# Four matmuls behind the MLP norm's mean, and a new order of the first loads, in a decoder trunk

## The chip, the cores and the metric

One core of a Trainium2 chip runs the whole kernel. Its engines are TensorE (PE, matmuls; PEld, its weight loads), VectorE (DVE), ScalarE (ACT), GpSimd (POOL) and SyncE (SP). Transfers between DRAM and SBUF are issued from the queues of SP, ACT and POOL. The metric is the device time of one execution in microseconds, lower is better, as the median of several runs.

## The reference

Two layers over 512 tokens of width 1024, in float32. Each layer is a mixer (latent attention in the first, gated linear attention in the second) and an MLP with a squared ReLU, each behind an RMS norm and added to the residual stream. The MLP is where most of the time goes:

```python
def rms_norm(x, gain):
    xf = x.astype(jnp.float32)
    y = xf * lax.rsqrt(jnp.mean(xf * xf, axis=-1, keepdims=True) + EPS)
    return (y * gain.astype(jnp.float32)).astype(x.dtype)
...
def sq_relu_mlp(xn, w_up, w_down):
    hid = jnp.square(jax.nn.relu(xn @ w_up))
    return hid @ w_down
...
for i in range(DEPTH):
    xn = rms_norm(x, norm_mix[i])
...
    x = x + mix.astype(x.dtype)
    x = x + sq_relu_mlp(rms_norm(x, norm_mlp[i]), mlp_w_up[i], mlp_w_down[i]).astype(x.dtype)
return rms_norm(x, final_norm)
```

w_up is 1024 x 4096 and w_down 4096 x 1024. The first projection of the attention layer multiplies the normed x by columns of `mla_w_in`.

## The kernel before

**Precision.** Every large product is made of three passes in the float32r format: each operand is split into a high part (ACT copies it with rounding, line 112) and a low part (DVE subtracts the high part, line 115). `mm3` (lines 120 to 122) is high x high, low x high and high x low with 512 moving columns; the MLP's `matmuls` (line 826) does the same with 256 columns. Each weight piece thus takes a transfer, an ACT split and a DVE subtraction before TensorE can use it.

**The start.** The end of `trunk_kernel` issues the first transfers: the gains, the weights of the latent projection in four parts of 256 KB (`raw0`, named wraw_ckv in the profile, by `load_part`), and x in eight tiles of 128 x 512 (256 KB each, by `load_x`, named xT). Some stand in SP's queue and some in ACT's. Eight counters are shared by the transfers of these two queues, so the ninth transfer in the program's order waits for the landing of the first, and so on. `exp_set` (line 127) loads ACT's function table. Fifteen matmuls on a tile of ones (line 1599, two passes each) come first on TensorE. The program's order is kept for ACT's splits: one weight part, then the two x tiles that go with it (line 245 makes the high part of x times its gain, line 246 on DVE the low part). The product over k = 0 to 7 uses x tile k with weight part k // 2, and TensorE takes the k in order. The product behind it needs the next weight transfer (wraw, 1 MB).

**The MLP.** `mlp` is a generator. Its first part runs while the projection ahead of it ends. Then it builds both matrix products by a seven-product scheme over 2 x 2 blocks: `up_block(b)` yields steps (`s1` with the product named 11, `s2` with 21, `s5` with T1 and so on), and `down_block` yields products over the hidden tiles. A list in `mlp` sets which step follows which. Moving operands are x0 to x7 (high `x0h`, low `x0l`), the combinations T0 to T3, and h, the split hidden tiles. Weights are wh and wl (three buffers each); for block 1's product 11 the pieces are the tiles w, which lie in the space of T3.

Where these tiles lie matters for the reading of the profile. In the program as built, the byte address within a partition, modulo 512, is 96 for all x and T tiles and for w, 416 for wh and wl, and 352 for h. An h1 tile is shifted by 40 elements for that, except the first of each down block, which stays unshifted at 192:

```python
h = dp.tile([P, 8 * TH + 40], F32R, tag="h1", name=uname("h"))
c = 0 if turn[1] != s else 40
h = h[:, c : c + 8 * TH].rearrange("p (i k t) -> p i k t", i=2, k=4)
```

Below, the offset of a matmul is the address of its moving tile less that of its weights, modulo 512 bytes. Two matmuls of offset 0, whose result is never read, already stand at the MLP's begin:

```python
x = quad["11"][0][0]
PE.matmul(t[:, h * TH : (h + 1) * TH], x[:, :P], x, start=h == 0, stop=True, skip_group_check=True)
```

**The norm.** The mean of squares is one float32 matmul with a constant matrix (`nrm.mean`, line 255, tile acc), kept in program order between block 1's product 11 and block 0's product 21. `nrm.finish` makes the reciprocal root from it, which the products need only at their evacuation.

Of the kernel before, what the change touches and what calls it, by code (L numbers as in the profile page):

```python
# [10 lines left out]
F32 = mybir.dt.float32  # L11
# [7 lines left out]
P = 128  # L19
# [6 lines left out]
TH = S // 2  # L26
# [23 lines left out]
def trunk_kernel(ctx: ExitStack, tc: tile.TileContext, t_in: dict, out: bass.AP, out_row: bass.AP):  # L50
    nc = tc.nc
    PE, ACT, DVE, POOL, SP = nc.tensor, nc.scalar, nc.vector, nc.gpsimd, nc.sync
# [6 lines left out]
    def opened(name, side="left", space=None):  # L59
        es = ExitStack()  # L60
        kw = {"space": space} if space is not None else {"side": side}
        now[name] = es, es.enter_context(tc.tile_pool(name=uname(name), bufs=1, reuse_waits="tile", **kw))
        return now[name][1]
# [4 lines left out]
    def pool_of(name):  # L68
        return now[name][1]
# [3 lines left out]
    def uname(s):  # L73
        count[0] += 1
        return f"{s}_{count[0]}"

    def bank(tag):
        if "mps" in now:
            return pool_of("mps").tile([P, 512], F32, tag="u", bufs=3, name=uname("ps"))
        return pool_of("ps").tile([P, 512], F32, tag=f"ps_{tag}", bufs={"a": 2, "b": 3, "c": 3}[tag], name=uname("ps"))  # L80
# [29 lines left out]
    def split(src, hi, lo, hi_eng=ACT, lo_eng=DVE, order=lambda i: i):  # L110
        if hi_eng is ACT:
            raised.append(order(ACT.activation(hi, src, AF.Copy)))  # L112
        else:
            hi_eng.tensor_copy(hi, src)
        return lo_eng.tensor_tensor(lo, src, f(hi), ALU.subtract)  # L115
# [10 lines left out]
    def exp_set():  # L126
        table[0] = tc.keep_in_program_order(ACT.preload_act_table_set("natural_log_exp_and_others"))
# [17 lines left out]
    def piece(raw, a, n, order=lambda i: i):  # L145
        hi = sb.tile([P, a, n], F32R, tag="wh", bufs=3, name=uname("wh"))
        lo = sb.tile([P, a, n], F32R, tag="wl", bufs=3, name=uname("wl"))
        cut_at.append(split(raw, hi, lo, order=order))
        return hi, lo
# [13 lines left out]
    xall = const.tile([P, ND, S], F32, name="xT")  # L163
    xT = [xall[:, j] for j in range(ND)]
    x_in = t_in["x"].rearrange("(j p) t -> p j t", p=P)

    def load_x(q, j):
        q.dma_start(xall[:, j], x_in[:, j])

    eps_t = const.tile([P, 1], F32, name="eps_t")  # L170
    DVE.memset(eps_t, EPS)
# [637 lines left out]
    def mlp(layer, nrm, nxt, final=False):  # L809
# [342 lines left out]
        mp = opened("mps", space=bass.MemoryType.PSUM)  # L1152
# [4 lines left out]
        for n, (m0, tk) in {2: (0, first), 3: (0, second), 4: (KH, first), 5: (KH, second)}.items():  # L1157
            acc[n] = xall[:, m0 : m0 + KH, tk]

        t = mp.tile([P, 512], F32, tag="seed", name=uname("ps"))  # L1160
        for h in range(2):
            x = quad["11"][0][0]
            PE.matmul(t[:, h * TH : (h + 1) * TH], x[:, :P], x, start=h == 0, stop=True, skip_group_check=True)
        for b in range(2):
            wide[b] = halves(wide_raw())
        for b, t in enumerate(halves(wide_raw())):
            fills[b](t)
        kept = tc.keep_in_program_order
        for b in range(2):
            blocks[b].pop(0)()  # L1170
        t = nrm.combine(KH - 1, dp.tile([P, 4, TH], F32, tag="q", bufs=6, name=uname("q")))
        kept(nrm.mean())
        made[1]["21"] = piece(made[1]["a12"], KH, 256)
        kept(cut_at[-1])
        kept(nrm.combined(KH - 1, t))
# [399 lines left out]
    raw0 = pool_of("stage").tile([P, ND, 256], F32, tag="wraw", bufs=2, name="wraw_ckv")  # L1575
    src0 = t_in["mla_w_in"][0][:, QL : QL + KL].rearrange("(k p) n -> p k n", p=P)

    def load_part(k0, k1):
        SP.dma_start(raw0[:, k0:k1], src0[:, k0:k1])

    ACT.dma_start(gains, t_in["gains"])
    load_part(0, 2)
    load_x(ACT, 0)
    load_x(SP, 1)
    load_x(ACT, 2)
    load_part(2, 4)
    load_x(ACT, 3)
    load_part(4, 6)
    load_x(ACT, 4)
    load_x(SP, 5)  # L1590
    load_part(6, 8)
    load_x(SP, 6)
    load_x(SP, 7)
    POOL.dma_start(pos_i, t_in["positions"])
    POOL.dma_start(invf, t_in["inv_freq"].to_broadcast([P, 32]))
    exp_set()
    warm = bank("c")
    for _ in range(15):
        PE.matmul(warm[:, :P], ones128, ones128, start=True, stop=True)
    w0 = []  # L1600
    for k0, k1 in ((0, 2), (2, 4), (4, 6), (6, 8)):
# [40 lines left out]
    n_mix1 = Mixer(ND, inv_d, "mix", ND, "A")  # L1642
    n_mlp0 = mlp_norm(0)
    mlp0 = mlp(0, n_mlp0, n_mix1)
    out_proj(t_in["mla_w_o"][0], O, n_mlp0, mlp0, begun)
    next(mlp0, None)
# [5 lines left out]
    class Final:  # L1652
# [39 lines left out]
        def row(self, t, c, p):  # L1692
# [19 lines left out]
            for eng, q, cs in ((ACT, ACT, slice(0, 384)), (DVE, SP, slice(384, D))):  # L1712
# [4 lines left out]
                q.dma_start(o[:, cs], y[:, cs])  # L1717

    mlp1 = mlp(1, n_mlp1, Final(), True)
    out_proj(t_in["gla_w_o"][0], Y, n_mlp1, mlp1)  # L1720
    next(mlp1, None)
# [23 lines left out]
def build(nc, shapes):  # L1745
    args = {}
    for name, (shape, dt) in shapes.items():
        args[name] = nc.dram_tensor(f"in_{name}_dram", shape, dt, kind="ExternalInput").ap()
    o = nc.dram_tensor("out_0_dram", (D, TH), F32, kind="ExternalOutput").ap()
    o_row = nc.dram_tensor("out_1_dram", (TH, D), F32, kind="ExternalOutput").ap()  # L1750
    with tile.TileContext(nc) as tc:
        trunk_kernel(tc, args, o, o_row)
# [22 lines left out]
```

## Time and profile before

| | |
|---|---|
| Median of 3 runs | 1066.10 us (1065.54 to 1068.97) |
| The profiled execution's own time | 1065.53 us |
| Its span, first to last instruction | 1063.8 us |
| TensorE busy | 1055.4 us, 99% |
| VectorE busy | 856.6 us, 81% |
| ScalarE busy | 642.4 us, 60% |
| Mean granted TensorE clock | 0.998 |
| First MLP's two spare matmuls, its mean | at 189.39 us, at 195.24 us |
| Second MLP's mean | at 742.27 us |

Time stamps are microseconds from the span's start. In a timeline row stand the start, the duration, the engine, the line, the operation, the result tile and its inputs (buffer numbers left out), the shapes, and how many like instructions the row merges; brackets hold the idle time before it and what ended it. Matmuls are pipelined: a record lasts longer than its step, so the pace is read from start to start, or from the number of matmuls in a stretch.

### The profile page before, as it was taken

The page shows a single profiled execution, that of the slowest core. Times are in us where ns is not written, and L with a number is a line of the kernel's source. Part 1 is how long each engine was busy: PE and PEld are TensorE (multiplying, and loading weights), DVE is VectorE, ACT ScalarE, POOL GpSimd, SP SyncE. Part 2 cuts the span into 40 slices and gives each one's busy share as a digit, 9 for nine tenths or more (in the row PEclk, how much of TensorE's full clock was granted, in tenths as well). Part 3 has the DMA queues.
Part 4 walks back from the last instruction along what each step waited for, and adds up shares of the span by engine and source line. Part 5 has one row for each costly group of instructions (what it writes and reads, how often), then busy time and mean ns, then how long its engine had stood idle before and what let it go on. Part 6 is the DMA issues. An engine that isn't in the chain of part 4 may idle for free.

```text
span 1063.8 us, 17962 instructions
## 1 busy us (share of the span) xinstructions
PE 1055.4 (99%) x7332; PEld 975.8 (92%) x7332; DVE 856.6 (81%) x1186; ACT 642.4 (60%) x937; POOL 78.8 (7%) x104
## 2 busy tenths in 40 slices
PE   9999999999999999999999999999999999999997
PEld 7788988999999999988788888888999999999986
DVE  6789879899799789967565654678999799799965
ACT  6577645575667777644334734655665667776734
POOL 7400001000000000030000000001000000000000
PEclk9999999999999999999999999999999999999999
DMA  7312017765553663360222211238665555654412
GB/s 219 91 50 80 7 34 217 165 193 145 173 141 118 179 155 112 99 203 26 53 77 80 80 59 61 80 99 218 179 141 154 158 126 159 173 127 117 139 40 79
DMA packets 114946, 127.81 MB, mean 120 GB/s; under 512 B 8640, under 2 KB 86736, under 8 KB 114864
## 3 DMA queue, kind: packets, MB, share of 16 engines
q1 hardware_dynamic: 98832, 108.15, 32.0%
q0 software_dynamic: 13792, 16.80, 10.2%
q10 hardware_dynamic: 2240, 1.73, 0.5%
q8 instruction: 57, 0.93, 0.4%
q14 instruction: 25, 0.20, 0.1%
HBM read 124.56 MB, written 2.10 MB: 119 GB/s over the span
## 4 chain that ended last, share of the span: by engine, by line
PE 96%; DVE 2%; ACT 0%; DMA 0%; issue 0%; ACTq 0%; DVEq 0%
PE ps L826 51%; PE ps L120 13%; PE ps L122 13%; PE ps L121 13%; PE ps L1426 2%; PE ps L137 1%; PE ps L1465 0%; PE ps L1432 0%; PE ps L1412 0%; PE ps L685 0%; PE ps L686 0%; PE ps L684 0%; PE ps L682 0%; PE ps L683 0%; DVE stat L695 0%; DMA gains<-in_gains_dram 0%
## 5 line engine op out<-in xcount | busy, mean ns | idle before, releaser
L112 ACT ACTIVATE wh<-raw 128x1024 fp32r<-128x1024 f32 x208 | 219.8, 1060 | 152.7 <-PE ps L826 99.4
L115 DVE TENSOR_TENSOR wl<-raw,wh 128x1024 fp32r<-128x1024 f32 x208 | 251.8, 1220 | 25.4 <-ACT wh L112 25.1
L826 PE MATMUL ps<-h,wh 128*128 128x256 f32 x1344 | 168.6, 278 | 0.0
L826 PEld LDWEIGHTS ps<-h,wh 128*128 128x128 f32 x1344 | 161.2, 188 | 0.0
L120 PE MATMUL ps<-set,wh 128*128 128x512 f32 x232 | 91.3, 394 | 0.0
L826 PE MATMUL ps<-h,wl 128*128 128x256 f32 x672 | 91.2, 278 | 0.0
L121 PE MATMUL ps<-set,wh 128*128 128x512 f32 x232 | 90.7, 391 | 0.1
L122 PE MATMUL ps<-set,wl 128*128 128x512 f32 x232 | 90.7, 391 | 0.0
L112 ACT ACTIVATE wh<-wraw 128x1024 fp32r<-128x1024 f32 x41 | 43.1, 1057 | 74.2 <-PE ps L122 41.5
L826 PEld LDWEIGHTS ps<-h,wl 128*128 128x128 f32 x672 | 83.6, 188 | 0.0
L879 POOL DMA_DIRECT2D raw<-in_mlp_w_up_dram x20 | 25.8, 1290 | 707.4 <-DMA raw<-in_mlp_w_up_dram 330.5
L891 ACT ACTIVATE q<-q 128x512 f32<-128x512 f32 x64 | 40.3, 630 | 40.2 <-DVE q L890 39.8
L115 DVE TENSOR_TENSOR h<-q,h 128x1024 fp32r<-128x1024 f32 x44 | 53.7, 1222 | 9.1 <-ACT h L112 9.0
L120 PE MATMUL ps<-wh,set 128*128 128x512 f32 x144 | 59.7, 414 | 0.0
L115 DVE TENSOR_TENSOR wl<-wraw,wh 128x1024 fp32r<-128x1024 f32 x41 | 50.3, 1226 | 11.1 <-ACT wh L112 10.8
L122 PE MATMUL ps<-wh,set 128*128 128x512 f32 x144 | 56.3, 391 | 0.0
L121 PE MATMUL ps<-wl,set 128*128 128x512 f32 x144 | 56.2, 390 | 0.0
L121 PEld LDWEIGHTS ps<-set,wh 128*128 128x128 f32 x232 | 43.6, 188 | 9.9 <-DVE set L246 0.9
L122 PEld LDWEIGHTS ps<-set,wl 128*128 128x128 f32 x232 | 43.6, 188 | 9.4 <-DVE wl L115 0.5
L120 PEld LDWEIGHTS ps<-set,wh 128*128 128x128 f32 x232 | 43.5, 188 | 9.0 <-issue 0.2
L112 ACT ACTIVATE h<-q 128x1024 fp32r<-128x1024 f32 x44 | 46.0, 1049 | 0.2
L121 PE MATMUL ps<-hl,wh 128*128 128x512 f32 x96 | 37.4, 389 | 0.0
(512 smaller groups left out, 2789.4 us busy)
## 6 DMA issues: line engine op xcount, KB each, us to landing
raw<-in_mlp_w_down_dram SPq DMA_DIRECT2D x38, 1024.0 KB, 5.2
raw<-in_mlp_w_up_dram SPq DMA_DIRECT2D x70, 512.0 KB, 5.3
wraw<-in_gla_w_in_dram SPq DMA_DIRECT2D x11, 1024.0 KB, 5.1
raw<-in_mlp_w_up_dram POOLq DMA_DIRECT2D x20, 512.0 KB, 7.4
raw<-in_mlp_w_down_dram POOLq DMA_DIRECT2D x6, 1024.0 KB, 9.3
wraw<-in_mla_w_o_dram SPq DMA_DIRECT2D x8, 512.0 KB, 4.8
wraw<-in_gla_w_o_dram SPq DMA_DIRECT2D x8, 512.0 KB, 4.7
wraw_qn<-in_mla_w_uq_dram SPq DMA_DIRECT2D x6, 256.0 KB, 3.4
```

What stands on the lines that cost most here:

```text
L112: raised.append(order(ACT.activation(hi, src, AF.Copy)))
L115: return lo_eng.tensor_tensor(lo, src, f(hi), ALU.subtract)
L120: PE.matmul(psum, wh, xh, start=start, stop=False, **kw)
L121: PE.matmul(psum, wh, xl, start=False, stop=False, **kw)
L122: PE.matmul(psum, wl, xh, start=False, stop=stop, **kw)
L137: PE.transpose(psum, src, ident[: src.shape[0], : src.shape[0]])
L826: return PE.matmul(p[:, m * TH : (m + 1) * TH], w[i][:, k - k0, m * P : (m + 1) * P], x[k][j], start=start, stop=stop, skip_group_check=True,)
L879: POOL.dma_start(t, rows(half, trail), accum_op=ALU.add)
L891: ACT.activation(qs, qs, AF.Square)
L1426: PE.matmul(p[:, t * 64 : (t + 1) * 64].rearrange("p (n c) -> p n c", c=m), k[:, sl], later, start=True, stop=True)
```

## The change

It does four things. Behind the mean of each MLP, four more matmuls of offset 0 on x0h go into an unused PSUM tile (`spare`, kept in program order). The last six x tiles are loaded in pairs, three transfers of 512 KB, one from ACT's queue and two from SP's; weight part 4 to 6 goes from SP's queue to ACT's. The function table's load moves ahead, between ACT's first x transfer and its second. The matmuls on ones go from 15 to 14.

```diff
@@ -164,8 +164,8 @@
     xT = [xall[:, j] for j in range(ND)]
     x_in = t_in["x"].rearrange("(j p) t -> p j t", p=P)
 
-    def load_x(q, j):
-        q.dma_start(xall[:, j], x_in[:, j])
+    def load_x(q, j, n=1):
+        q.dma_start(xall[:, j : j + n], x_in[:, j : j + n])
 
     eps_t = const.tile([P, 1], F32, name="eps_t")
     DVE.memset(eps_t, EPS)
@@ -1157,19 +1157,24 @@
         for n, (m0, tk) in {2: (0, first), 3: (0, second), 4: (KH, first), 5: (KH, second)}.items():
             acc[n] = xall[:, m0 : m0 + KH, tk]
 
-        t = mp.tile([P, 512], F32, tag="seed", name=uname("ps"))
-        for h in range(2):
+        def spare(t, n):
             x = quad["11"][0][0]
-            PE.matmul(t[:, h * TH : (h + 1) * TH], x[:, :P], x, start=h == 0, stop=True, skip_group_check=True)
+            for h in range(n):
+                i = PE.matmul(t[:, h * TH : (h + 1) * TH], x[:, :P], x, start=h % 2 == 0, stop=True, skip_group_check=True)
+                if n > 2:
+                    kept(i)
+
+        kept = tc.keep_in_program_order
+        spare(mp.tile([P, 512], F32, tag="seed", name=uname("ps")), 2)
         for b in range(2):
             wide[b] = halves(wide_raw())
         for b, t in enumerate(halves(wide_raw())):
             fills[b](t)
-        kept = tc.keep_in_program_order
         for b in range(2):
             blocks[b].pop(0)()
         t = nrm.combine(KH - 1, dp.tile([P, 4, TH], F32, tag="q", bufs=6, name=uname("q")))
         kept(nrm.mean())
+        spare(mp.tile([P, 4 * TH], F32, tag="d", bufs=2, name=uname("ps")), 4)
         made[1]["21"] = piece(made[1]["a12"], KH, 256)
         kept(cut_at[-1])
         kept(nrm.combined(KH - 1, t))
@@ -1575,27 +1580,24 @@
     raw0 = pool_of("stage").tile([P, ND, 256], F32, tag="wraw", bufs=2, name="wraw_ckv")
     src0 = t_in["mla_w_in"][0][:, QL : QL + KL].rearrange("(k p) n -> p k n", p=P)
 
-    def load_part(k0, k1):
-        SP.dma_start(raw0[:, k0:k1], src0[:, k0:k1])
+    def load_part(k0, k1, q=SP):
+        q.dma_start(raw0[:, k0:k1], src0[:, k0:k1])
 
     ACT.dma_start(gains, t_in["gains"])
     load_part(0, 2)
     load_x(ACT, 0)
     load_x(SP, 1)
-    load_x(ACT, 2)
+    exp_set()
+    load_x(ACT, 2, 2)
     load_part(2, 4)
-    load_x(ACT, 3)
-    load_part(4, 6)
-    load_x(ACT, 4)
-    load_x(SP, 5)
+    load_part(4, 6, ACT)
+    load_x(SP, 4, 2)
     load_part(6, 8)
-    load_x(SP, 6)
-    load_x(SP, 7)
+    load_x(SP, 6, 2)
     POOL.dma_start(pos_i, t_in["positions"])
     POOL.dma_start(invf, t_in["inv_freq"].to_broadcast([P, 32]))
-    exp_set()
     warm = bank("c")
-    for _ in range(15):
+    for _ in range(14):
         PE.matmul(warm[:, :P], ones128, ones128, start=True, stop=True)
     w0 = []
     for k0, k1 in ((0, 2), (2, 4), (4, 6), (6, 8)):
```

TensorE at the mean of the first MLP; ps with a number is the PSUM tile, acc the sum of squares, w, x and wh as above. Before:

```order
L826 MATMUL ps_2303<-x1h_2030,w_2172 128x256 x2
L826 MATMUL ps_2303<-x2h_2118,w_2172 128x256 x2
L826 MATMUL ps_2303<-x3h_2226,w_2172 128x256 x2
L255 MATMUL ps_2336<-acc_1947,inv_101 128x512
L826 MATMUL ps_2274<-x4h_1950,wh_2163 128x256
L826 MATMUL ps_2274<-x4l_1951,wh_2163 128x256
```

Now:

```order
L826 MATMUL ps_2299<-x1h_2026,w_2168 128x256 x2
L826 MATMUL ps_2299<-x2h_2114,w_2168 128x256 x2
L826 MATMUL ps_2299<-x3h_2222,w_2168 128x256 x2
L255 MATMUL ps_2332<-acc_1943,inv_101 128x512
L1163 MATMUL ps_2334<-x0h_1939 128x256 x4
L826 MATMUL ps_2270<-x4h_1946,wh_2159 128x256
L826 MATMUL ps_2270<-x4l_1947,wh_2159 128x256
```

The four stand between the mean and product 21; all other matmuls of the MLP keep their order and their addresses modulo 512.

ACT at the start. Before:

```order
L1581 DMA gains<-in_gains_dram 128x51
L168 DMA xT<-in_x_dram 128x512 x4
L127 ACT_TABLE_LOAD
L112 ACTIVATE wh_149<-wraw_ckv 128x512
L245 ACTIVATE set_153<-xT,gains 128x512
L245 ACTIVATE set_157<-xT,gains 128x512
```

Now:

```order
L1586 DMA gains<-in_gains_dram 128x51
L168 DMA xT<-in_x_dram 128x512
L127 ACT_TABLE_LOAD
L168 DMA xT<-in_x_dram 128x2x512
L1584 DMA wraw_ckv<-in_mla_w_in_dram 128x2x256
L112 ACTIVATE wh_145<-wraw_ckv 128x512
L245 ACTIVATE set_149<-xT,gains 128x512
```

The table load is ahead of the pair x2 and x3. The transfer that waits for the landing of the gains is now a weight part instead of x4; ACT's splits keep their order.

SP at the start. Before:

```order
L1579 DMA wraw_ckv<-in_mla_w_in_dram 128x2x256
L168 DMA xT<-in_x_dram 128x512
L1579 DMA wraw_ckv<-in_mla_w_in_dram 128x2x256 x2
L168 DMA xT<-in_x_dram 128x512
L1579 DMA wraw_ckv<-in_mla_w_in_dram 128x2x256
L168 DMA xT<-in_x_dram 128x512 x2
L142 DMA wraw_321<-in_mla_w_in_dram 128x8x256
```

Now:

```order
L1584 DMA wraw_ckv<-in_mla_w_in_dram 128x2x256
L168 DMA xT<-in_x_dram 128x512
L1584 DMA wraw_ckv<-in_mla_w_in_dram 128x2x256
L168 DMA xT<-in_x_dram 128x2x512
L1584 DMA wraw_ckv<-in_mla_w_in_dram 128x2x256
L168 DMA xT<-in_x_dram 128x2x512
L142 DMA wraw_317<-in_mla_w_in_dram 128x8x256
```

Two transfers of x became pairs, one weight part left the queue, and the 1 MB weight transfer (wraw) is the seventh of this queue instead of the ninth. Only the second pair and wraw still wait for a landing (that of the first weight part and that of x0).

## The prediction

> **What bounds the kernel now.** I read the page first (engines, then the chain that ended last).
>
> ```profile
> PE 1055.4 (99%) x7332; PEld 975.8 (92%) x7332; DVE 856.6 (81%) x1186; ACT 642.4 (60%) x937; POOL 78.8 (7%) x104
> PE 96%; DVE 2%; ACT 0%; DMA 0%; issue 0%; ACTq 0%; DVEq 0%
> ```
>
> TensorE is never off for long, so the end can move in only two ways: the matmuls follow each other faster, or the short start and the few stalls shrink. Busy time cannot show the first, because a busy TensorE need not run at its best pace. So I asked for the matmuls of the MLP (line 826, all 128x256) stretch by stretch.
>
> ```profile
> 197.00:238.00 41.00, 41.00 (x350) 41.00 (x349) 1.00 0.60 160
> 247.00:325.00 78.00, 78.00 (x664) 78.00 (x663) 1.00 0.58 160
> 335.00:390.00 55.00, 55.00 (x488) 55.00 (x487) 1.00 0.50 140
> 400.00:460.00 60.00, 60.00 (x532) 60.00 (x531) 1.00 0.41 121
> 744.00:785.00 41.00, 41.00 (x350) 41.00 (x350) 1.00 0.60 160
> 882.00:936.00 54.00, 54.00 (x479) 54.00 (x478) 1.00 0.53 147
> ```
>
> Columns: stretch, length, busy TensorE and number of matmuls, busy weight loads, granted clock, DMA. A record lasts 0.28 us and one that reaches into a stretch is counted, so a step is (length + 0.28) / count: 78.28 / 664 = 117.9 ns in the second row, 60.28 / 532 = 113.3 ns in the fourth. Same line, shape, granted clock (1.00) and full occupation, and two paces, 4.5 ns apart. The first MLP runs at 117.9 ns up to about 332 us and at 113.3 after it; the second repeats it (41.28 / 350 = 117.9, then 54.28 / 479 = 113.3). Each pace holds for tens of microseconds: it is a state that something sets. The timeline of TensorE shows where.
>
> ```profile
> 189.39 0.40 PE L1163 MATMUL ps<-x0h 128*128 128x256 f32 x2
> 189.62 0.28 PE L826 MATMUL ps<-x0h,wh 128*128 128x256 f32 x1
> 190.09 0.28 PE L826 MATMUL ps<-x1h,wh 128*128 128x256 f32 x1
> 190.54 0.28 PE L826 MATMUL ps<-x2h,wh 128*128 128x256 f32 x1
> ...
> 192.36 0.28 PE L826 MATMUL ps<-x0h,w 128*128 128x256 f32 x1
> 192.84 0.28 PE L826 MATMUL ps<-x1h,w 128*128 128x256 f32 x1
> ...
> 195.24 1.02 PE L255 MATMUL ps<-acc,inv 128*128 128x512 f32 x2
> 195.69 0.68 PE L826 MATMUL ps<-x4h,wh 128*128 128x256 f32 x1
> 196.21 0.28 PE L826 MATMUL ps<-x4l,wh 128*128 128x256 f32 x1
> 196.56 0.28 PE L826 MATMUL ps<-x5h,wh 128*128 128x256 f32 x1
> 197.03 0.28 PE L826 MATMUL ps<-x6h,wh 128*128 128x256 f32 x1
> ```
>
> Four matmuls lie between the starts of x1h and x2h: (190.54 - 190.09) / 4 = 113 ns, the fast pace, right behind the two spare matmuls of line 1163. In the product with the tile w a step is (192.84 - 192.36) / 4 = 120 ns. Behind the mean (line 255) it is (197.03 - 196.56) / 4 = 118 ns, and so it stays. I sort matmuls by the offset between the addresses of their moving tile and their weights, modulo 512 bytes, as the build assigns them: 0 for line 1163 and for the product with w, 192 for x and T against wh or wl, 448 for an ordinary h, 288 for the first h1 tile of a down block, which `operand` leaves unshifted. What the rows show: offset 0 draws to 120 ns; offsets 192 and 448 run at 113.3 or 117.9, whichever they were left in; and the entry behind the mean leaves the slow one. The pace turns once more:
>
> ```profile
> 331.20 0.63 PE L826 MATMUL ps<-h,wl 128*128 128x256 f32 x4
> 331.67 0.28 PE L826 MATMUL ps<-x4h,wh 128*128 128x256 f32 x1
> 332.13 0.28 PE L826 MATMUL ps<-x5h,wh 128*128 128x256 f32 x1
> ...
> 396.54 0.74 PE L826 MATMUL ps<-h,wl 128*128 128x256 f32 x5
> 397.12 0.28 PE L826 MATMUL ps<-x4h,wh 128*128 128x256 f32 x1
> 397.60 0.28 PE L826 MATMUL ps<-x5h,wh 128*128 128x256 f32 x1
> ```
>
> Those unshifted h1 blocks of 48 products stand at 238.5 to 244.1, 326.1 to 331.7 and 391.5 to 397.1. Entered slow, the first ends slow and the second ends fast. The third is entered fast and ends fast. They run at 5.6 us / 48 = 117 ns in either state.
>
> **The change part by part: the mean.** Four matmuls of offset 0, on x0h as weights and moving tile, go behind the mean of each MLP. They wait for nothing (x0h was read at 189.39, the PSUM tile is unused), and nobody reads them. Cost: 4 x 120 ns (the w rows) = 0.48 us in each MLP, 0.96 together, all on TensorE's path. DVE and ACT meanwhile go on with the weights that come next.
>
> What they bring is a state, and no row shows this very sequence, so I bound it. At worst the state stays slow: nothing gained. At best everything from 196.6 to 331.7 runs fast: 135.1 us less the two unshifted blocks of 5.6 each = 123.9 us / 117.9 ns = 1051 matmuls x 4.5 ns = 4.7 us in each MLP, 9.4 together. I take the fast end. The nearest rows are those at 189.39: two matmuls of offset 0, then offset 192, and the pace is fast. The mean itself only ends late (the start of 196.21 less one step is 196.09), so the first of the four starts like any matmul behind a stall. A fast entry into the first unshifted block then resembles the third block, which ends fast.
>
> [...]
>
> Can DVE and ACT keep up?
>
> ```profile
> 196.00:240.00 44.00, 44.00 (x374) 43.91 (x373) 40.67 (x42) 29.34 (x38) 1.28 (x1) 1.00 0.62 163
> ```
>
> DVE has 40.67 us of work there. At the fast pace the 44 us become 44 x 113.3 / 117.9 = 42.3, so DVE would be 96% full: tight, but below full, and the four matmuls give it 0.48 us of lead. I cost this at nothing; uncovered, it is a rival below.
>
> **The start.** Queues, table load and warm-up are one term, since they feed one chain: transfers, ACT, DVE, TensorE.
>
> ```profile
> 4.22 1.28 ACT L127 ACT_TABLE_LOAD   x1 [4.22 <-DMA gains<-in_gains_dram]
> 5.52 0.63 ACT L112 ACTIVATE wh<-wraw_ckv 128x512 fp32r<-128x512 f32 x1
> 6.05 1.33 ACT L245 ACTIVATE set<-xT,gains 128x512 fp32r<-128x512 f32 x2
> 8.10 0.71 ACT L245 ACTIVATE set<-xT,gains 128x512 fp32r<-128x512 f32 x1
> 10.06 0.73 ACT L245 ACTIVATE set<-xT,gains 128x512 fp32r<-128x512 f32 x1 [1.25 <-DMA xT<-in_x_dram]
> ...
> 5.90 0.94 PE L1599 MATMUL ps<-ones 128*128 128x128 f32 x7
> 6.81 0.73 PE L120 MATMUL ps<-set,wh 128*128 128x512 f32 x2
> 17.70 0.39 PE L120 MATMUL ps<-set,wh 128*128 128x512 f32 x1
> 18.60 0.39 PE L121 MATMUL ps<-set,wh 128*128 128x512 f32 x1
> 19.03 0.50 PE L122 MATMUL ps<-set,wl 128*128 128x512 f32 x1
> ...
> 10.82 0.75 DVE L246 SCALAR_TENSOR_TENSOR set<-xT,gains,set 128x512 fp32r<-128x512 f32 x1 [1.10 <-ACT set L245]
> 17.66 2.70 DVE L115 TENSOR_TENSOR wl<-wraw,wh 128x1024 fp32r<-128x1024 f32 x2 [1.74 <-ACT wh L112]
> ...
> 7.00:8.00 1.00, 0.94 (x4) 0.46 (x4) 1.00 (x2) 0.82 (x2) 0.00 (x0) 1.00 0.54 58
> 9.00:10.00 1.00, 1.00 (x6) 0.81 (x5) 0.71 (x2) 0.00 (x0) 0.42 (x1) 1.00 1.07 401
> ```
>
> ACT's last x transfer waits for the landing of the gains, the table load follows it, and the first split follows that at 5.52. Now the table load runs during that wait; behind the wait ACT issues one weight transfer (some 0.4 us) and can split at about 4.3. Then it needs x0, which is in by 6.05 at the latest. One warm-up matmul less (two passes; 0.91 us for the seven from 5.90 to 6.81, so 0.13 each) takes the other bound of the first product back by 0.26: TensorE begins some 0.3 us earlier. SP issues two transfers fewer and no longer stands behind x's landings before its third weight transfer; what lands when is still set by the bytes ahead in the queues. The first product needs x in order, and x2 now shares one transfer, and one landing, with x3. Before, x2 was in by 8.10 and x3 only by 10.06: in ACT's queue the same bytes stand ahead of x3's end, and the hole at 7 to 8 us (58 GB/s against 401 two microseconds later) lies in front of it. So x2 lands with x3, at about 10.0. Then ACT takes 0.73, DVE 0.75, and TensorE gets x2's low part at 11.5. From there stand 35 matmuls of this product (one of x2's six done, five blocks of six behind) and two of the next; a step is (18.60 - 17.70) / 4 = 0.225 us, so 37 x 0.225 = 8.3, and the matmul that starts at 19.03 today starts at 19.8: +0.8 us. If the transfer lands a microsecond sooner, that matmul only waits for wl (17.66 + 1.35) as it does now, and the start costs nothing. The low end, -0.3, has that weight transfer sooner too and takes TensorE's whole earlier beginning; the high end, +1.3, has x2 at 10.5. I take +0.8, since x3's row is the nearest.
>
> The Trainium skill ("DMA: Bandwidth & Descriptors", section "Issuing engines are not separate DMA queues") says that transfers from ACT and SP share the same 16 engines and that a second issuing queue saves issue time only. The 401 GB/s with both queues full agrees: moving a weight transfer to ACT's queue brings no bandwidth.
>
> **Sum.** Against the profiled run: 1065.5 - 9.4 + 1.0 + 0.8 = 1057.9. That run lies 0.6 under the median of 1066.1, so I forecast 1058.5 for a median.
>
> **Rivals.**
> - The state stays slow behind the four matmuls, or pace is set by columns alone. For it: the stall at the mean leaves slow today. Against: offset 0 led to fast at 189.39. Time: 1066.1 + 1.0 + 0.8 = 1067.9, no measurable change.
> - Fast only until the first unshifted block, whose end at 244.1 was slow although 331.7 and 397.1 were fast. Gain 42 us less the four matmuls, 41.5 / 117.9 ns x 4.5 ns = 1.6 per MLP: 1066.1 - 3.2 + 1.8 = 1064.7.
> - The other side: the slow state survives, and its new phase makes the second and third unshifted blocks end slow too, as the first does today. Place: 331.7. Then 332 to 462 us, less one block, also runs slow: 124 us / 113.3 ns x 4.5 ns = 4.9 per MLP: 1067.9 + 9.8 = 1077.7. It decides as soon as the matmuls behind 331.7 step at 118 ns.
> - DVE becomes the bound between 196 and 332 us and eats half: 1058.5 + 4.7 = 1063.2.
>
> **Chances.** Fast throughout 0.70 (own range 1056.5 to 1060.5: start -0.3 to +1.3, a few tenths to one microsecond lost to DVE); fast to the first block 0.09; state unchanged 0.12; slow beyond 0.06; DVE 0.03. A measurement here tells 0.3%, 3.2 us, from no change. Faster: the first and half of the last, 0.72. Same: 0.09 + 0.12 + 0.01 = 0.22. Slower: 0.06. A range to 1065.5 takes in the partial cases and leaves out the unchanged and the slower one.
>
> **What the changed profile would show.** Between 197 and 238 us line 826 at 113.3 ns (about 364 matmuls in 41 us) and no turn at 332; the same behind the second mean; four rows at line 1163 of 115 to 120 ns each behind line 255. The first x2 set of ACT behind a DMA wait at about 10 us, and TensorE idle then. Wrong: 117.9 ns behind the mean, or DVE as releaser of weight loads there; a start gain, if x2's set stands near 8 us.

## The result, and the profile after

The changed kernel takes 1059.2 us (median of 6 runs, 1058.46 to 1061.33) against 1065.88 us before on the same chip: ratio 0.9937, 95% interval 0.9922 to 0.9952. That is 6.7 us or 0.6% less, 0.7 us more than the 1058.5 forecast. The profiled execution took 1058.69 us.

The page's first part and its chain look like before's: TensorE is as full, and there is just less of it.

```profile
PE 1047.2 (99%) x7338; PEld 967.7 (92%) x7338; DVE 855.7 (81%) x1186; ACT 640.9 (61%) x937; POOL 78.8 (7%) x104
PE 96%; DVE 2%; DMA 1%; issue 0%; ACT 0%; ACTq 0%; DVEq 0%
```

Six more matmuls in all, and 8.2 us less busy time. Line 826 stretch by stretch, columns as in the prediction:

```profile
197.00:238.00 41.00, 40.48 (x358) 40.60 (x359) 1.00 0.63 163
247.00:325.00 78.00, 78.00 (x690) 78.00 (x689) 1.00 0.60 161
335.00:390.00 55.00, 55.00 (x487) 55.00 (x486) 1.00 0.52 139
400.00:460.00 60.00, 59.35 (x524) 59.16 (x522) 1.00 0.38 115
744.00:785.00 41.00, 41.00 (x363) 41.00 (x363) 1.00 0.55 158
882.00:936.00 54.00, 54.00 (x478) 54.00 (x477) 1.00 0.59 152
```

The second row had 664 matmuls and has 690, the fifth had 350 and has 363: 78.28 / 690 = 113.4 ns and 41.28 / 363 = 113.7. The rows behind 332 us were fast already and stay so. (The first row starts ahead of the first product; the fourth ends behind the last one.) TensorE's timeline at the first mean:

```profile
195.94 0.40 PE L826 MATMUL ps<-x3h,w 128*128 128x256 f32 x2
196.18 1.02 PE L255 MATMUL ps<-acc,inv 128*128 128x512 f32 x2
196.64 1.04 PE L1163 MATMUL ps<-x0h 128*128 128x256 f32 x4
197.52 0.28 PE L826 MATMUL ps<-x4h,wh 128*128 128x256 f32 x1
197.99 0.28 PE L826 MATMUL ps<-x5h,wh 128*128 128x256 f32 x1
198.44 0.28 PE L826 MATMUL ps<-x6h,wh 128*128 128x256 f32 x1
198.89 0.28 PE L826 MATMUL ps<-x7h,wh 128*128 128x256 f32 x1
```

The four spares take 0.88 us, of which about 0.40 is the mean's late end, which x4h's first matmul bore before. Behind them the steps are (197.99 - 197.52) / 4 = 118 ns once, and then (198.89 - 198.44) / 4 = 113: the pace is fast after four matmuls, and no later block of offset 288 ends it. DVE in the tightest stretch:

```profile
196.00:240.00 44.00, 44.00 (x384) 43.52 (x384) 40.96 (x43) 30.01 (x39) 1.27 (x1) 1.00 0.65 167
```

DVE is 93% full, and no weight load between 197 and 332 us waits for it.

The start, first ACT's timeline:

```profile
4.37 0.63 ACT L112 ACTIVATE wh<-wraw_ckv 128x512 fp32r<-128x512 f32 x1 [1.28 <-DMA wraw_ckv<-in_mla_w_in_dram]
6.03 1.33 ACT L245 ACTIVATE set<-xT,gains 128x512 fp32r<-128x512 f32 x2 [1.03 <-DMA xT<-in_x_dram]
10.00 1.33 ACT L245 ACTIVATE set<-xT,gains 128x512 fp32r<-128x512 f32 x2 [2.12 <-DMA xT<-in_x_dram]
```

TensorE's two waits in its timeline:

```profile
10.78 0.50 PE L120 MATMUL ps<-set,wh 128*128 128x512 f32 x1 [0.62 <-ACT set L245]
11.56 0.50 PE L121 MATMUL ps<-set,wh 128*128 128x512 f32 x1 [0.29 <-DVE set L246]
```

And two windows (length; busy TensorE, weight loads, DVE, ACT, POOL; clock; DMA share, GB/s):

```profile
7.00:8.00 1.00, 0.94 (x5) 0.46 (x4) 1.00 (x2) 0.88 (x2) 0.00 (x0) 1.00 1.19 54
9.00:12.00 3.00, 2.09 (x9) 1.19 (x8) 1.24 (x2) 1.33 (x2) 1.81 (x4) 1.00 1.06 388
```

The first split stands at 4.37, not 5.52, but then ACT waits for x0 to 6.03 and the first product begins at 6.80 as before. x2's set waits for the pair to 10.00, and TensorE is idle 0.91 of the 3 us from 9 to 12. The hole of 54 GB/s is still there.

Matched matmul by matmul with before, TensorE is 0.96 us late at 20 us and stays so up to the mean; each set of four spares adds 0.47 net; the first MLP then gains 4.65 us between 197 and 332, the second 4.66. The last matmul is 7.4 us earlier. Behind it the changed kernel takes 0.55 us longer. The larger part is a wait in DVE's last small steps (in its timeline, before and then now):

```profile
1058.85 0.15 DVE L1708 SCALAR_TENSOR_TENSOR sm<-sm 128x1 f32<-128x1 f32 x1
1059.12 0.22 DVE L1709 SCALAR_TENSOR_TENSOR sm<-sm,sm 128x1 f32<-128x1 f32 x1
```

```profile
1051.45 0.15 DVE L1710 SCALAR_TENSOR_TENSOR sm<-sm 128x1 f32<-128x1 f32 x1
1052.07 0.22 DVE L1711 SCALAR_TENSOR_TENSOR sm<-sm,sm 128x1 f32<-128x1 f32 x1 [0.47 <-DVE sm L1710]
```

The step from one to the other takes 0.62 us instead of 0.27; the rest lies behind the issue of the last output transfers. This is not chance from run to run. From the last matmul's start to the span's end, the seven profiled kernels with the old loads take 6.60 to 6.61 us, and the six with the new loads of x and of the weight parts take 7.17 to 7.21. So it goes with the new loads, although nothing in this part of the program was edited; how they reach it was not tried. Sum: 0.96 + 0.94 - 9.31 + 0.55 = -6.86, against 1058.69 - 1065.53 = -6.84.

### The profile page after: what moved, and what is told of

It reads as the page before. It is cut to its first block, busy times and chain, and to the rows that moved or that the text cites. A ratio compares the mean times of both kernels' runs of the same rounds, so it can differ in the third digit from the quotient of the medians.

```text
span 1057.0 us, 17970 instructions
## 1 busy us (share of the span) xinstructions
PE 1047.2 (99%) x7338; PEld 967.7 (92%) x7338; DVE 855.7 (81%) x1186; ACT 640.9 (61%) x937; POOL 78.8 (7%) x104
## 4 chain that ended last, share of the span: by engine, by line
PE 96%; DVE 2%; DMA 1%; issue 0%; ACT 0%; ACTq 0%; DVEq 0%
PE ps L826 51%; PE ps L120 13%; PE ps L121 13%; PE ps L122 13%; PE ps L1431 2%; PE ps L137 1%; DMA xT<-in_x_dram 1%; PE ps L1470 0%; PE ps L1437 0%; PE ps L1417 0%; PE ps L685 0%; PE ps L686 0%; PE ps L682 0%; PE ps L684 0%; PE ps L683 0%; DVE stat L695 0%
```

## The experiments

Each is timed against the kernel before on the same chip, in three groups of four; before was 1066.01, 1065.76 and 1066.05 us in them.

### The two halves apart

**spares_only:** the kernel before, with `spare` and its two calls as in the diff above.

> The kernel before with the four matmuls behind each mean and nothing else. By position in the program, the changed kernel's TensorE falls 0.96 us behind at the start and then gains 8.35 us in the two MLPs (4.65 us each, less 0.47 us for the four matmuls). Theory (the spares carry the whole gain and the start costs): 1065.9 - 8.3 = 1057.6 us, 1.5 us faster than the full change; line 826 at 113.3 ns between 197 and 238 us, and x2's set near 8 us. Rival (the two traces' start differs only from run to run, or the new start helps): 1059.2 us or more, the same as the full change.

Measured: 1057.62 us (1057.29 to 1058.07), ratio 0.9918 (0.9905 to 0.9931). Line 826 in its trace:

```profile
247.00:325.00 78.00, 78.00 (x690) 78.00 (x690) 1.00 0.59 161
744.00:785.00 41.00, 41.00 (x363) 41.00 (x363) 1.00 0.55 155
```

The eight matmuls alone bring 8.4 us, more than the whole change. Its start is before's, and yet its TensorE is 0.52 us later at 20 us than in before's profiled run. So the start varies from run to run: at that point the other profiled kernels with before's start unaltered stand from 0.09 us ahead of it (before_h1_448) to 0.38 (spares_448) and 0.60 us (two_spares_448) behind it. Against the mean of these five, the new start costs some 0.7 us there, not 0.96.

**start_only:** the changed kernel without the second call.

```diff
         kept(nrm.mean())
-        spare(mp.tile([P, 4 * TH], F32, tag="d", bufs=2, name=uname("ps")), 4)
```

> The changed kernel without the four matmuls: queues, pairs, table load and warm-up alone. Theory: the start costs what it cost in the full change, 0.96 us at the matmul that waited for wl at 19.03 us before: 1066.8 us; 117.9 ns behind the mean. Rival (the start is worth nothing or a gain): 1065.9 us or below.

Measured: 1068.77 us, ratio 1.002 (1.0012 to 1.0029). Line 826 in its trace:

```profile
197.00:238.00 41.00, 41.00 (x348) 40.97 (x348) 1.00 0.63 161
247.00:325.00 78.00, 78.00 (x665) 78.00 (x663) 1.00 0.61 162
```

The slow pace, as before. The start is a loss. The profiled run (1067.06) is 1.5 us over before's: 0.93 at the last matmul and 0.59 behind it, as in the changed kernel. By the median the loss is larger: three of the 11 runs lie at 1067.1 to 1067.2, eight at 1068.2 to 1070.7. What can make that difference shows in the next experiment.

### What sets the pace behind the mean

**spares_at_192:** the changed kernel, the spares' weights 80 elements further on.

```diff
             x = quad["11"][0][0]
+            c = 80 if n > 2 else 0
...
-                i = PE.matmul(..., x[:, :P], x, ...)
+                i = PE.matmul(..., x[:, c : c + P], x, ...)
```

> The changed kernel with the weights of the four spares taken 80 elements further on in x0h, so that their offset is 192 like that of the products around them; number, shape, place and operands' tile stay. Theory (offset 0 moves the phase between weight load and matmul): the state stays slow, 117.9 ns up to 332 us, 1059.2 + 9.3 = 1068.5 us. Rival (any four matmuls between the mean and product 21 do it, by taking up the stall or the weights): 1059.2 us.

Measured: 1062.21 us (1061.9 to 1064.54), ratio 0.9964 (0.9952 to 0.9975): between the two. Line 826:

```profile
197.00:238.00 41.00, 39.84 (x339) 39.74 (x338) 1.00 0.62 151
247.00:325.00 78.00, 78.00 (x690) 78.00 (x689) 1.00 0.62 162
```

At the mean the theory holds: four matmuls of the same tile, shape and place, but of offset 192, leave the pace at 117.8 ns (41 us less the part ahead of the first product). Then the first block of offset 288, which ended slow before, ended fast. That turn I had not expected here.

The same profiled run, taken at 1064.54 us, shows the start's second cost: TensorE's wait for x2 in its timeline.

```profile
11.85 0.49 PE L120 MATMUL ps<-set,wh 128*128 128x512 f32 x1 [1.79 <-ACT set L245]
```

The windows behind it, columns as above:

```profile
13.00:14.00 1.00, 1.00 (x4) 0.81 (x3) 0.79 (x2) 1.00 (x3) 0.92 (x3) 0.53 1.09 354
14.00:15.00 1.00, 1.00 (x3) 0.73 (x3) 1.00 (x3) 1.00 (x3) 1.00 (x2) 0.50 1.05 338
15.00:16.00 1.00, 1.00 (x4) 0.79 (x3) 1.00 (x2) 1.00 (x3) 0.86 (x2) 0.50 0.69 230
16.00:17.00 1.00, 1.00 (x5) 0.82 (x4) 1.00 (x2) 0.42 (x1) 0.97 (x2) 0.77 0.07 24
```

x2 came 1.1 us later than in the changed kernel's profiled run, TensorE stood idle for 1.79 us, and from about 13.1 to 16.5 the granted clock was 0.50: 3.4 us at half pace, 1.7 us lost. one_spare and three_at_192, with the same start, show it too (idle 1.66 and 1.99 of the 3 us from 9 to 12, clock 0.50 at 14 to 15); the kernel before, the changed kernel's profiled run (idle 0.91) and start_only's (0.36) do not. The two groups of runs of start_only, and the changed kernel's two runs at 1060.7 and 1061.3 beside four at 1058.5 to 1059.5, are some 2 us apart, which fits. Those runs have no profile, but the mean granted clock of each run is on record: in start_only 0.998 to 0.999 in the three and 0.996 to 0.998 in the eight, where 3.4 us at half would take 0.0016. The old start is not free of it either, by the same sign: two of before's 20 runs in this group, at 1068.8 and 1069.5 us, have 0.997. The Trainium skill ("TensorE: Matmul & The Clock Gate", section "HAM oscillation — how this bites in real kernels") asks for no idle gap over some 3.4 us. Here the clock fell 1.2 us behind a gap of 1.79 us, so the measurement decides.

**one_spare:** the changed kernel with `spare(..., 1)`.

> The changed kernel with one spare matmul instead of four behind each mean. In the changed trace the start of the weight load ahead of each matmul stands 115, 116, 117 and 118 ns before its matmul from the second spare to the first product of 21: each product of offset 0 adds 1 ns, and the kernel before stays slow at 114.5. Theory (the phase must be carried past about 116): with one spare the first product meets 115 ns as before, the state stays slow: 1059.2 + 9.3 - 0.7 = 1067.8 us. Rival (one matmul of offset 0 is enough to set the state): 1059.2 - 0.7 = 1058.5 us.

Measured: 1062.99 us (1061.49 to 1065.73), ratio 0.9967 (0.9955 to 0.9978). By the trace the same picture as with four at 192: slow behind the mean (x350 in 744:785), the first block of offset 288 ends fast (x690 in 794:872). One spare does not set the pace, as the theory said; the time was 4.8 us under its number because that block ended fast, which brings 2 x 690 x 4.44 ns = 6.1 us, and the half clock, which its profiled run shows, takes up to 1.7 of it back.

**two_spares_448:** spares_448 (below) with two spares.

> Old start, every h1 shifted (no block of offset 288, so nothing later can turn the pace), and two spares of offset 0 instead of four behind the mean. In the changed trace the weight load stands 115, 116, 117 and 118 ns ahead of the second, third, fourth spare and the first product of 21; with two spares the first product stands at 116. Theory A (one step past the 115 of the slow pattern is enough): fast from the mean on, 1057.1 - 4 x 0.12 = 1056.6 us. Theory B (the phase must be carried to 118, so that all four are needed): slow to the end of both MLPs, 2 x 2304 x 4.44 ns = 20.5 us: 1077.1 us.

Measured, 12 runs: three at 1056.1, 1056.5 and 1056.7 us, nine from 1064.9 to 1067.1, none at 1077. Neither theory: with two spares it is open in each execution, and the nine are 8.3 to 11.0 us over the three, which fits one slow MLP (10.2 us). Those runs have no profile, but a mean granted clock of 0.998 or 0.999, so it is not the half clock. The profiled run, at 1056.66, is fast in both MLPs. In it the first product's weight load stands 114 ns ahead, not the expected 116, and two matmuls later 110 ns, as in the fast stretches; so in this run no phase carried past 115 set the pace. Two stand on the edge. With four, the 32 runs of the seven kernels that have them spread by at most 2.9 us in each, less than a slow first part of one MLP (4.65 us) would add.

### The blocks of offset 288

In the slow stretch the trace's weight loads go in threes: in the kernel before 120 of the 364 between mean and block last 192 ns, every third, nearly all others 187 or 188. In the fast stretch none does. The block itself has two patterns: steps of 116, 117, 117 ns, which keep the weight load 114 to 115 ns ahead of its matmul, and steps of 116, 118, 120, 113, which carry it from 111 to 118 ns. It ends slow from the first and fast from the second. Whether a slow entry leads to the one or the other looked like a matter of where in the three the block begins.

**three_at_192:** spares_at_192 with three.

> The changed kernel with three spares of offset 192 instead of four. In the slow state every third weight load lasts 192 ns instead of 188. In the kernels that left the first block of offset 288 slow (before, start_only) a long load stands just ahead of the block; 361 and 364 matmuls behind the mean, as against 360, it doesn't, and the block ended fast. Theory (what decides is where in the pattern of three the block begins): three spares give 363 = 360 + 3, the block begins behind a long load and ends slow, 117.8 ns to 332 us: 1062.2 - 0.2 + 2 x 690 x 4.44 ns = 1068.1 us. Rival (any matmul between the mean and product 21 makes the first block end fast): 1062.0 us.

Measured: 1069.96 us (1069.28 to 1073.12), ratio 1.0042 (1.003 to 1.0055). Line 826:

```profile
247.00:325.00 78.00, 78.00 (x665) 78.00 (x664) 1.00 0.61 161
```

One matmul fewer than in spares_at_192, and 7.75 us more, of which 2 x 690 x 4.44 ns = 6.1 is the pace: the first block ends slow again in both MLPs, and the pace turns at the second, as before. The number of matmuls between the mean and the block decides: 360 (before, start_only) and 363 end slow, 361 (one_spare) and 364 (spares_at_192) fast, in both MLPs of each. No count with a remainder of two by three was tried. Of the 1.9 us over the forecast the half clock at the start, which its profiled run shows, can have 1.7.

**before_h1_448:** the kernel before, no block of offset 288.

```diff
-                    c = 0 if turn[1] != s else 40
+                    c = 40
```

> The kernel before with every h1 tile shifted by 40 elements, so that the blocks of offset 288 become blocks of offset 448. Theory (the only thing that turns the pace to fast in the kernel before is the block of offset 288 at 326 us): the slow pace stays to the end of each MLP, (528 + 576) x 4.44 ns = 4.9 us more, and three blocks of 48 at 117.8 instead of 116.7, 0.2 us: 2 x 5.1 = 10.2 us slower, 1076.2 us. Rival (the turn comes from something else there, such as the second half of the down product): fast from 332 us on, and the blocks faster by 48 x 3.4 ns each where it is fast: 1065.7 us.

Measured: 1075.74 us (1075.51 to 1077.07), ratio 1.0095 (1.0081 to 1.0109).

```profile
335.00:390.00 55.00, 55.00 (x469) 55.00 (x468) 1.00 0.49 139
```

469 matmuls instead of 488: the slow pace goes to the MLP's end. So the turn at 332 us in the kernel before was those blocks' work, and nothing else in 266 us of MLP ends the slow pace.

**spares_448:** spares_only with the same line.

> The kernel before with the four spares of offset 0 behind the mean, the old start, and every h1 tile shifted by 40 elements: no block of offset 288 is left, and none is needed since the state is fast from the mean on. Theory: six blocks of 48 at 113.3 instead of 116.7 ns, 6 x 48 x 3.4 = 0.98 us, and no slow steps behind them (some 15 ns each): 1057.6 - 1.1 = 1056.5 us. Rival (without those blocks the pace falls back to 117.8 somewhere): 1058 to 1067 us.

Measured: 1057.11 us (1056.51 to 1057.57), ratio 0.9917 (0.9904 to 0.9931). With the pace set at the mean, the same edit that cost 10.0 us costs nothing, and in the profiled runs the last matmul stands 1.2 us sooner than in spares_only (9.0 against 7.8 us ahead of before); by the medians it is 0.5 us, within what the two groups can tell apart.

### The start

**x2_x3_apart:** the changed kernel.

```diff
-    load_x(ACT, 2, 2)
+    load_x(ACT, 2)
+    load_x(ACT, 3)
```

> The changed kernel with x2 and x3 as two transfers of 256 KB on ACT's queue instead of one of 512 KB; the rest of the new start stays. Theory (the pair makes TensorE wait for x2, and the wait, some 1.5 to 2 us long, at times takes the granted clock down to 0.5 for 3 us): x2's set near 8.5 us, no gap of over 1 us, granted clock 1.00 from 9 to 20 us in the profiled run, and 1059.2 - 1.4 = 1057.8 us with the runs within 1 us of each other. Rival (another part of the new start costs it, the part 4 to 6 in ACT's queue or the pairs on SP's): 1059.2 us, scattered over some 3 us as the changed kernel's runs.

Measured: 1058.56 us (1058.07 to 1059.55), ratio 0.9933 (0.992 to 0.9947).

```profile
9.27 0.72 ACT L245 ACTIVATE set<-xT,gains 128x512 fp32r<-128x512 f32 x1 [0.97 <-DMA xT<-in_x_dram]
10.71 0.72 ACT L245 ACTIVATE set<-xT,gains 128x512 fp32r<-128x512 f32 x1 [0.72 <-DMA xT<-in_x_dram]
```

x2 comes 0.7 us before the pair did, TensorE waits 0.26 us for it and 0.29 for its low part, the clock stays at 1.00 and no run is over 1059.6. Of the 1.4 us 0.6 came. What the theory said of the clock fits, but x2's sooner landing bought nothing here: at 12 us TensorE stands 0.67 us ahead of the changed kernel's, and from 14 us on 0.30 behind it. What is shorter is the part behind the last matmul (6.74 us instead of 7.17). ACT's timeline shows the rival at work too, the weight part 4 to 6 in ACT's queue:

```profile
12.52 0.63 ACT L112 ACTIVATE wh<-wraw_ckv 128x512 fp32r<-128x512 f32 x1 [1.08 <-DMA wraw_ckv<-in_mla_w_in_dram]
13.05 1.32 ACT L245 ACTIVATE set<-xT,gains 128x512 fp32r<-128x512 f32 x2
```

Before, that split stood at 10.69 and x4's set at 11.38. Here, in start_only and in the changed kernel ACT waits for this part to 12.2 or 12.5, and x4's set follows at 12.7 to 13.1. In start_only, where x2's set stands at 9.05, TensorE is 0.37 us late at 12 us and 1.33 at 14: there the wait for this part makes the loss. Moving only this part back to SP's queue was not tried.

**old_start_invf_later:** spares_448, with the small transfer of `invf` issued behind x7's split.

```diff
-    POOL.dma_start(invf, t_in["inv_freq"].to_broadcast([P, 32]))
...
             nrm.scaled(j, xT[j], tc.keep_in_program_order)
+    POOL.tensor_copy(invf, f(nrm.out[7][0])[:, :32])
+    POOL.dma_start(invf, t_in["inv_freq"].to_broadcast([P, 32]))
```

> spares_448 with the transfer of invf (POOL's queue, 16 KB to 128 partitions) issued only when x7 has been split, by a copy on POOL that reads that tile. Theory (this transfer makes the hole of 58 GB/s at 7 to 8 us): no hole there, x3's set about 1 us sooner, some 0.6 us less at the start: 1056.5 us; the hole moves to some 17 to 21 us, where weights of 1 MB land with time to spare. Rival (the hole is the queues' own, or comes back in front of wraw): 1057.1 us or up to 1 us more. The tables that hang on invf are used at 57 us and were ready at 41, so they stay hidden.

Measured: 1055.96 us (1055.58 to 1056.45), ratio 0.9908 (0.9893 to 0.9922), the fastest here.

```profile
7.00:8.00 1.00, 0.94 (x4) 0.48 (x3) 1.00 (x2) 0.83 (x3) 0.00 (x0) 1.00 1.07 370
```

ACT's timeline:

```profile
7.96 1.46 ACT L245 ACTIVATE set<-xT,gains 128x512 fp32r<-128x512 f32 x2
9.96 1.34 ACT L245 ACTIVATE set<-xT,gains 128x512 fp32r<-128x512 f32 x2
```

370 GB/s where before had 58 and spares_448, which differs from this run by the invf edit alone, 79: 16 KB to 128 partitions on POOL's queue made the hole. x2 and x3 are split together at 7.96, x3 some 1.4 us sooner, and the matmul that waited for wl starts at 18.49 instead of 19.03.

**new_start_invf_later:** the changed kernel with both edits (every h1 shifted, `invf` later).

> The changed kernel with every h1 shifted and invf later. Theory (the pair of x2 and x3 is late because the hole lies in front of it): x2's set near 8.5 us, no gap on TensorE over 0.7 us, granted clock 1.00 to 20 us, 1056.5 us and runs within 1 us of each other; then the new start is as good as the old. Rival (a transfer of 512 KB lands late whatever stands in front of it): x2's set at 9.5 us or later, 1058 us.

Measured: 1057.26 us (1057.06 to 1058.0), ratio 0.992 (0.9907 to 0.9932).

```profile
9.39 1.34 ACT L245 ACTIVATE set<-xT,gains 128x512 fp32r<-128x512 f32 x2 [1.74 <-DMA xT<-in_x_dram]
```

Without the hole the pair still lands at 9.4 and ACT waits 1.74 us for it: the rival. The runs lie within 1 us, as the theory had it. With the hole gone in both, the new start is 1.3 us slower than the old; in the profiled runs 0.9 of it stands at the last matmul and 0.6 behind it.

**old_loads_table_early:** spares_448 with the table load between ACT's first and second x transfer and 14 matmuls on ones.

> spares_448 with one part of the new start: the function table between ACT's first and second x transfer, and 14 matmuls on ones; the loads stay as before. Theory (the table is a gain for the first product alone, and x3's landing sets the end of it): the first product some 0.4 us sooner, TensorE idle as much longer ahead of x3, 1057.1 us, no change. Rival (the table load at 4.2 us held up the start): 1056.6 us.

Measured: 1057.75 us (1057.67 to 1058.74), ratio 0.9925 (0.9913 to 0.9937), 0.6 us over spares_448. ACT's queue:

```profile
1.84 3.84 ACTq L168 DMA_DIRECT2D xT<-in_x_dram  x3
5.73 0.63 ACT L112 ACTIVATE wh<-wraw_ckv 128x512 fp32r<-128x512 f32 x1 [2.63 <-DMA xT<-in_x_dram]
...
9.35 0.63 ACT L112 ACTIVATE wh<-wraw_ckv 128x512 fp32r<-128x512 f32 x1 [1.76 <-DMA wraw_ckv<-in_mla_w_in_dram]
```

No sooner first product. With the table load out of the way ACT's last x transfer waits for the landing of an x tile, to 5.7, instead of the gains', to 4.2; the split behind it stands where it stood, and the second weight part came 1.8 us later than before. So the early table alone buys nothing; whether it does where a weight part stands at that place, as in the new start, was not timed.

## Why the prediction was right, and where it was off

- **The pace as a state, and four matmuls of offset 0 to set it (-9.4): right.** Measured -9.31. spares_only shows that they do it alone, spares_at_192 that their offset does it and not their being there, and one and two spares that fewer do not do it reliably. There was luck in the number: the rows it was read from, at 189.39, have two spares, and two behind the mean settle it in 3 of 12 runs. The rival that columns alone set the pace falls with the rows above: same line, same shape, 113.4 and 117.9 ns.
- **The four matmuls' price (+0.48 per MLP): right.** 0.47 net.
- **The first block of offset 288, entered fast, ends fast: right.** Fast in 247:325. The rival that it ends slow rested on 244.1, which was a slow entry.
- **The other side, slow beyond 332 us:** it did not come. Its price (4.9 us per MLP) is measured: with those blocks gone, before_h1_448 lost 10.0 us in two MLPs. Its mechanism, a second and third block that end slow, is in no trace: every profiled run that has these blocks is fast behind 332 us. What decides the end of the first block, entered slow, is in the runs the number of matmuls ahead of it in threes, not a loose phase.
- **DVE did not become the bound.** It was 93% full where I had worked out 96.
- **The start (+0.8): the side was right, the account in part wrong.** x2 with x3 at 10.00 and x2's low part on TensorE at 11.56 are as forecast; the 37 matmuls from there took 0.231 us each instead of 0.225, so the matmul of 19.03 came at 20.12, +1.1 (0.96 at 20 us). That comparison flatters the kernel before, whose profiled start was an early one; against the mean of five it is some 0.7. "TensorE begins some 0.3 us earlier" did not hold in the profiled run, where x0 kept ACT waiting to 6.03 (6.05 had been its bound), and held in start_only, 0.38 us; it matters little, since later landings set the end. I overlooked that the weight part 4 to 6, which now waits for the gains' landing in ACT's queue, comes late as well, and that a longer idle of TensorE can go with a lower clock.
- **The step that failed: nothing was put down for the end.** The sum ends with the start's term, as if the new loads acted at the start alone. They also go with 0.55 us behind the last matmul.
- **Sum:** for the profiled run 1057.9 against 1058.69. Of the 0.8 us the end is 0.55 and the start 0.16. By the medians, 1059.2 - 1057.62 = 1.6 us lie between spares_only and the whole change; in the profiled runs it is 1.0, of which 0.44 at the last matmul and 0.54 behind it, and two of the changed kernel's six runs are 1.3 us or more over the other four.

## What to carry to other kernels

A TensorE that is 99% busy can still have two paces for one instruction; count matmuls per stretch before believing a busy share, and look where the pace turns. Where it hangs on how the stream is entered, a few unread matmuls of the right operand addresses behind the interruption can be worth ten times their price; take a number of them that every run answers alike. At a start, look at when each piece lands and not at the number of transfers: here two tiles in one transfer made the first wait for the second, a weight part moved to another queue came late, and a small transfer spread over all partitions held up large ones. Compare starts over several profiled runs, for the same start stood up to 0.7 us apart in five of them. And follow the comparison to the last instruction: an edit at the start came with half a microsecond at the end.

## What the runs showed of the hardware that was not expected

- The offset of moving tile and weights modulo 512 bytes goes with the pace of 128x256 matmuls: 119 to 120 ns at 0, 116.7 at 288, and 113.3 or 117.8 at 192 and 448 by the way of entry. What in the chip makes it so stays open.
- The slow pace repeats every three matmuls, and one matmul more or less ahead of a block of offset 288 decided the pace of the 82 us behind it, in both MLPs.
- With two spares the same program took 1056.1 or some 1066 us from one execution to the next. Why it tips there stays open.
- Idle time of 1.7 us or more of TensorE within 3 us was followed by 3.4 us at a granted clock of 0.50 in all three profiled runs that had it; 0.9 us was not.
- The order of the first loads goes with the time behind the last matmul, 6.6 or 7.2 us, a millisecond later. Why stays open.
- A transfer of 16 KB to 128 partitions on POOL's queue held the rate at 58 to 79 GB/s for a microsecond in which the same loads without it moved 370.
